# A hybrid trunk layer on one core: later turns of gated tiles, and queries and chain outputs turned by DMA

## The chip, the core and the metric

The kernel runs on one core of a Trainium2 chip. The metric is the device time of one execution in microseconds (us); for the kernel before it is the median of three runs. The profile comes from one more execution, taken by the hardware profiler. Engines are named as in the profile: PE (TensorE, matrix products and transposes), DVE (VectorE), ACT (ScalarE), POOL (GpSimd) and SP (SyncE, which here only issues loads).

## The reference, cut to what matters

The layer takes x (256 x 2048, float32) through three sub-layers, each with an RMS norm before and after it: a SwiGLU half-step, a mixer of two gated linear attentions, a second SwiGLU half-step.

```python
def swiglu(x, w_gate, w_up, w_down):              # w_gate, w_up: 2048 x 5504
    return (jax.nn.silu(x @ w_gate) * (x @ w_up)) @ w_down

proj = u @ w_in
(g_q, g_k, g_v, g_out, g_code, h_q, h_f, h_i, h_out, z_gla, z_hgrn) = jnp.split(proj, offsets, axis=-1)
...
o_gla = merge_heads(rms_norm(o_gla, gla_norm)) * jax.nn.silu(g_out)       # 4 heads, dk 128, dv 256
...
o_hgrn = merge_heads(rms_norm(o_hgrn, hgrn_norm)) * jax.nn.silu(h_out)    # 8 heads, dk 128, dv 128
merged = (jax.nn.sigmoid(z_gla + b[0]) * (o_gla @ w_branch_gla)
          + jax.nn.sigmoid(z_hgrn + b[1]) * (o_hgrn @ w_branch_hgrn))
return merged @ w_out
```

Both attentions are causal recurrences with a decay for each key channel: S_t = diag(a_t) S_{t-1} + k_t v_t^T, o_t = S_t^T q_t.

## The kernel before, in words

**Tiles.** The 256 rows are two row tiles t = 0, 1 of 128 partitions; columns go in blocks of CB = 512. A product needs its left operand transposed, with the contracted dimension on the partitions, so whatever is a left operand later has to be turned (128x128 transposes, four for a 128x512 tile). Every float32 operand is split in a high part (`hi`, rounded, by ACT) and the rest (`lo`, by DVE; `split_into`, line 152), and a product is three matmuls on PE (`mm3`, line 157, lines 159 to 161). Weights come as chunks of 128x1024 elements: `raw` loaded by SP (line 135), `whi` by ACT (line 153), `wlo` by DVE (line 155), in a ring of five buffers. Some pairs of chunks are multiplied by a scheme of seven products (`seven`, line 263), which saves PE work and costs DVE sums.

**Two ways to turn a tile.** By PE: `transpose4` (line 397) writes four transposes (line 399) to a PSUM tile, from which ACT copies or splits. By DMA: `turn` (line 406) has ACT part the two 16-bit halves of each float32 into `halves` (line 410) and issue a transposing DMA from ACT's own queue (line 414); `joined` (line 417, instruction at 419) has ACT put the halves together again. Before the change DMA turns the gated tiles of both SwiGLU stages (`finish`, line 719) and the merged tiles of the mixer (`merge`, line 1262); PE turns all else, the queries (`transposed`, line 847) and the attentions' outputs (line 1006) among them.

**The order of the work.** The code is one long list of products, with small steps between them. `Side` (line 43) keeps two lists of generators. After a chunk of products the code calls `side.pump()`: each generator of the light list makes one step (to its next `yield`), and up to two of the heavy list, which holds the attention chains, make one as well. In a pair block called with `late` the heavy ones step only while the light list is empty; otherwise, with two or more of them, at every second pump. In `gemm_pair` (line 331) heavy steps stop (`side.full`) from the step before the first `seven` to the end of the block. `side.flush()` runs the light list out, `side.until(...)` pumps until something is there. Each engine then works through its own queue in a fixed order.

**The mixer** (line 800). One block for the GLA query, one for the code and the first HGRN query (line 1134), then pair blocks: GLA key and value, value and gate, gate and HGRN forget, HGRN value and gate of group 0, query and forget of group 1, value and gate of group 1. Six attention chains (`attention`, line 891) run beside them: GLA for t = 0, 1 (two output blocks each), HGRN group 0 and group 1 for t = 0, 1 (one each). A chain waits for its operands, goes through seven levels, for t = 0 turns its key (`ke`), then for each output block makes the products, the state, the norm and the gated output `on` (line 1001); two steps later PE turns `on` and it is split into `oT` (lines 1012, 1013). Then come the gate blocks and branches: `done("g")` (line 1247) pumps until the GLA outputs are there, gate block, two GLA branch blocks, `done("h")` (line 1253, group 0 alone), three gate blocks with two GLA branch blocks in between, then all chains are run out (line 1278). Four HGRN branch blocks (line 1280) each spawn `merge` for both row tiles: a product and a sum on DVE (lines 1264, 1265), four pumps, the turn, a load of a tile kept in DRAM (`h<-away`, line 1269, also from ACT's queue), four pumps, `joined`, one pump, the split. The output projection (`out_proj`, line 552, PSUM tiles `acc`) reads the result.

**The SwiGLU stages** (`ffn`, line 693). Eleven column blocks of gate and up products; for each, `finish` makes the gated tile, and one step later turns it, six steps later joins it in `hT`. The down projection (`down_proj`, line 605) reads `hT` as its left operand in 43 chunks for each half of the columns; after the second chunk it runs the light list out (line 662).

## Time and profile before

| | us |
|---|---|
| median of 3 runs | 2063.67 (2061.78 to 2066.02) |
| the profiled execution | 2067.03 |
| its span, first to last instruction | 2065.2 |

A line of the profile's groups or waits names an engine, a line of the kernel, the operation and the tiles (out<-in, with buffer numbers left out). Busy time is the time in which an engine carries out instructions; "idle before" is how long it stood still just ahead of them, and the arrow names what it waited for. `ACTq` and `SPq` are the queues of ACT and SP issuing a DMA; such issues are not counted as busy. Matmuls overlap on PE, so the distance between their starts, not the duration of one, is what PE pays.

### The profile page before, as it was taken

The numbers are of one execution on the slowest core, as the hardware profiler recorded it, in microseconds if no ns is written. First come the engines' busy times: TensorE is split into PE (matmuls) and PEld (weight loads), VectorE is DVE, ScalarE is ACT, GpSimd is POOL, SyncE is SP. The second block draws the span as 40 slices with busy tenths as digits, with TensorE's granted clock in tenths as the row PEclk, the third lists the DMA queues.
The fourth block names the chain that finished last, engine by engine and source line by source line (L and its number), as shares of the span: only waits on it lengthen the run. The fifth ranks groups of instructions, "written<-read, shape, count | busy, mean of one in ns | idle before, by whom it ended". The sixth has DMA issues, their size and how long they took to land. (4 is left out here: it accounts for less than half of the span.)

```text
span 2065.2 us, 28965 instructions
## 1 busy us (share of the span) xinstructions
PE 2046.2 (99%) x10299; PEld 1697.1 (82%) x10299; DVE 1864.5 (90%) x2195; ACT 1324.6 (64%) x1734; POOL 41.0 (2%) x87
## 2 busy tenths in 40 slices
PE   9999999999999999999999999999999999999998
PEld 8888888888888888878888887788888888888886
DVE  7999999998999889989999895578999999999897
ACT  7666666666666576576655556566666666766663
POOL 1000000000000100000000000010000000000000
PEclk9999999999999999999999999999999999999999
DMA  8777677677767566565665668956767767776664
GB/s 258 217 208 244 191 221 219 209 225 210 232 187 235 155 199 220 155 191 175 184 197 186 191 219 197 255 160 195 235 193 215 220 213 228 222 234 199 208 195 145
DMA packets 255129, 425.60 MB, mean 206 GB/s; under 512 B 71988, under 2 KB 80375, under 8 KB 254984
## 3 DMA queue, kind: packets, MB, share of 16 engines
q1 hardware_dynamic: 195472, 401.80, 61.8%
q10 hardware_dynamic: 59512, 21.94, 5.8%
q8 instruction: 81, 1.33, 0.3%
q14 instruction: 64, 0.52, 0.1%
HBM read 406.11 MB, written 4.19 MB: 199 GB/s over the span
## 5 line engine op out<-in xcount | busy, mean ns | idle before, releaser
L155 DVE TENSOR_TENSOR wlo<-raw,whi 128x1024 fp32r<-128x1024 f32 (+3 forms) x494 | 578.3, 1186 | 76.0 <-ACT whi L153 72.3
L153 ACT ACTIVATE whi<-raw 128x1024 fp32r<-128x1024 f32 (+3 forms) x494 | 499.3, 1025 | 193.3 <-PE c L160 59.0
L159 PE MATMUL c<-whi,xhi 128*128 128x512 f32 (+1 forms) x1270 | 494.8, 390 | 0.7 <-ACT whi L153 0.7
L161 PE MATMUL c<-wlo,xhi 128*128 128x512 f32 (+1 forms) x1270 | 491.5, 387 | 0.0
L160 PE MATMUL c<-whi,xlo 128*128 128x512 f32 (+1 forms) x1270 | 491.3, 387 | 0.0
L245 DVE TENSOR_TENSOR wlo<-raw,whi 128x1024 fp32r<-128x1024 f32 x256 | 304.0, 1219 | 36.0 <-ACT whi L284 22.8
L159 PEld LDWEIGHTS c<-whi,xhi 128*128 128x128 f32 x1270 | 238.4, 188 | 48.3 <-ACT whi L153 1.0
L161 PEld LDWEIGHTS c<-wlo,xhi 128*128 128x128 f32 x1270 | 238.4, 188 | 47.7 <-DVE wlo L245 0.2
L160 PEld LDWEIGHTS c<-whi,xlo 128*128 128x128 f32 x1270 | 238.5, 188 | 46.2
L284 ACT ACTIVATE whi<-raw 128x1024 fp32r<-128x1024 f32 x128 | 135.2, 1056 | 219.2 <-DVE raw L245 115.0
L245 DVE TENSOR_TENSOR wsuml<-wsum,wsumh 128x1536 fp32r<-128x1536 f32 x128 | 224.3, 1753 | 7.6 <-ACT wsumh L286 7.6
L161 PE MATMUL c<-wlo,hkhi 128*128 128x512 f32 x542 | 211.0, 389 | 0.0
L159 PE MATMUL c<-whi,hkhi 128*128 128x512 f32 x542 | 211.0, 389 | 0.0
L160 PE MATMUL c<-whi,hklo 128*128 128x512 f32 x542 | 210.9, 389 | 0.0
L282 ACT ACTIVATE wsumh<-wsum 128x1024 fp32r<-128x1024 f32 x128 | 134.6, 1052 | 84.2 <-DVE wsum L245 60.2
L280 ACT ACTIVATE whi<-raw 128x1024 fp32r<-128x1024 f32 x128 | 134.6, 1051 | 60.0 <-PE c L160 43.4
L245 DVE TENSOR_TENSOR wsum<-raw,raw 128x1024 f32<-128x1024 f32 x128 | 156.3, 1221 | 12.0 <-DMA raw<-in_ffn_w_down_dram 9.6
L161 PEld LDWEIGHTS c<-wlo,hkhi 128*128 128x128 f32 x542 | 101.7, 188 | 21.6 <-DVE wlo L245 0.3
L160 PEld LDWEIGHTS c<-whi,hklo 128*128 128x128 f32 x542 | 101.7, 188 | 21.0
L159 PEld LDWEIGHTS c<-whi,hkhi 128*128 128x128 f32 x542 | 101.7, 188 | 21.0
L245 DVE TENSOR_TENSOR c<-c,psum 128x512 f32<-128x512 f32 x135 | 87.4, 694 | 6.7 <-PE c L161 6.5
L245 DVE TENSOR_TENSOR wsum<-raw 128x512 f32<-128x512 f32 x128 | 88.4, 691 | 3.5
(326 smaller groups left out, 3192.2 us busy)
## 6 DMA issues: line engine op xcount, KB each, us to landing
raw<-in_ffn_w_down_dram SPq DMA_DIRECT2D x120, 512.0 KB, 4.8
raw<-in_w_in_dram SPq DMA_DIRECT2D x104, 512.0 KB, 4.5
raw<-in_ffn_w_gate_dram SPq DMA_DIRECT2D x90, 512.0 KB, 4.6
raw<-in_ffn_w_up_dram SPq DMA_DIRECT2D x90, 512.0 KB, 4.5
raw<-in_ffn_w_gate_dram SPq DMA_DIRECT2D x140, 256.0 KB, 3.9
raw<-in_ffn_w_up_dram SPq DMA_DIRECT2D x140, 256.0 KB, 3.7
raw<-in_w_in_dram SPq DMA_DIRECT2D x128, 256.0 KB, 3.6
raw<-in_ffn_w_down_dram SPq DMA_DIRECT2D x104, 256.0 KB, 4.0
```

The lines of the kernel that those rows point to most:

```text
L153: last[0] = nc.scalar.activation(hi, src, AF.Copy)
L155: nc.vector.tensor_tensor(lo, src, hi.bitcast(F32), op=ALU.subtract)
L159: nc.tensor.matmul(ps, lhsT=xhi, rhs=whi, start=start, stop=False)
L160: nc.tensor.matmul(ps, lhsT=xlo, rhs=whi, start=False, stop=False)
L161: nc.tensor.matmul(ps, lhsT=xhi, rhs=wlo, start=False, stop=stop)
L245: return nc.vector.tensor_tensor(o, x, y, op=op)
L280: nc.scalar.activation(ahi, ra, AF.Copy)
L282: nc.scalar.activation(hi[:, 0:2, :], wsum[:, 0:2, :], AF.Copy)
L284: nc.scalar.activation(bhi, rb, AF.Copy)
```

## The change

- `turn` is parted in `halved` (the 16-bit halves, on ACT or DVE) and `turn` (the DMA alone); `joined` can run on either engine as well.
- `finish`: the turn begins one step later for t = 0 and three for t = 1, and `joined` comes eight steps after the turn, not six.
- `down_proj`: no flush after the second chunk of the first half; a pump after each chunk instead, and a flush at the half's end.
- `turned_into`: a query tile is turned by DMA, 2 + 2t steps after it is spawned, and joined six steps after that. It takes the place of `transposed` for the GLA queries and the first HGRN queries.
- `attention`: all outputs but those of HGRN group 1 are turned by DMA one step after `on`, and joined and split four steps later.
- `merge`: both copies run on DVE, `halved` at once; the DMA goes out 3 + 2t steps later, `joined` and the split follow six steps after that.

```diff
-    def turn(src, halves):
+    def move(eng, dst, src):
+        if eng is nc.scalar:
+            nc.scalar.activation(dst, src, AF.Copy)
+        else:
+            eng.tensor_copy(dst, src)
+
+    def halved(src, halves, eng=nc.scalar):
 
         w = src.shape[-1]
         halves = halves.bitcast(U16)[:, :2 * w]
-        nc.scalar.activation(halves.rearrange("p (h f) -> p h f", h=2),
-                             src.bitcast(U16).rearrange("p (f h) -> p h f", h=2), AF.Copy)
+        move(eng, halves.rearrange("p (h f) -> p h f", h=2),
+             src.bitcast(U16).rearrange("p (f h) -> p h f", h=2))
+        return halves
+
+    def turn(halves):
         turned = work.tile([P, 8, P], U16, tag="tmp", name=nm("turned"), bufs=3)
-        turned = turned[:, :2 * w // P, :]
+        turned = turned[:, :halves.shape[-1] // P, :]
         nc.scalar.dma_start_transpose(turned, halves)
         return turned
...
@@ down_proj
-                if not hf and kt == 1:
-                    side.flush()
+                if not hf:
+                    side.pump()
                 kt += 1
             if not hf:
+                side.flush()
...
@@ finish
-                turned = turn(s[:, :w], fwork.tile([P, CB], F32, tag="halves", name=nm("halves")))
-                for _ in range(6):
+                for _ in range(1 + 2 * t):
+                    yield
+                halves = fwork.tile([P, CB], F32, tag="halves", name=nm("halves"))
+                turned = turn(halved(s[:, :w], halves))
+                for _ in range(8):
                     yield
...
@@ mixer
+            def turned_into(dst, src, before):
+
+                for _ in range(before):
+                    yield
+                turned = turn(halved(src, blk("halves")))
+                for _ in range(6):
+                    yield
+                joined(tiles4(dst), turned)
+                mark(dst)
...
-                    side.spawn(transposed(src, dsts[-1]))
+                    side.spawn(turned_into(dsts[-1], src, 2 + 2 * t) if dma else
+                               transposed(src, dsts[-1]))
...
@@ attention
                     yield
-                    yield
-                    tp = ps_tile()
-                    transpose4(tp, on)
+                    if (br, b0) == ("h", 1):
+                        yield
+                        tp = ps_tile()
+                        transpose4(tp, on)
+                    else:
+                        tp = on
+                        turned = turn(halved(on, blk("halves")))
+                        for _ in range(4):
+                            yield
+                        joined(tiles4(on), turned)
...
-            qT = spawn_T(qs, "qT")
+            qT = spawn_T(qs, "qT", True)
...
-            hqT = spawn_T(hqs, "hqT")
+            hqT = spawn_T(hqs, "hqT", True)
...
@@ merge
-                for _ in range(4):
+                halves = halved(s, blk("halves"), nc.vector)
+                for _ in range(3 + 2 * t):
                     yield
-                turned = turn(s, blk("halves"))
+                turned = turn(halves)
                 nc.scalar.dma_start(m, away[t][n])
-                for _ in range(4):
+                for _ in range(6):
                     yield
-                joined(tiles4(s), turned)
-                yield
+                joined(tiles4(s), turned, nc.vector)
```

## The prediction, made before the changed kernel was run

> **What bounds the kernel now.** I read the page first: who is busy, and how much is left.

> ```profile
> span 2065.2 us, 28965 instructions
> ...
> PE 2046.2 (99%) x10299; PEld 1697.1 (82%) x10299; DVE 1864.5 (90%) x2195; ACT 1324.6 (64%) x1734; POOL 41.0 (2%) x87
> ```

> PE stands idle for 2065.2 - 2046.2 = 19.0 us in all, so it is the bound. Time can come from two places alone: instructions taken off PE, and those 19 us. The waits of PE (total, times, longest) and two stretches of the windows view (length, then busy time of PE, PEld, DVE, ACT) say where the idle time is.

> ```profile
> PE acc L159 <- ACT whi L153: 4.4, 2, 2.8
> ...
> PE acc L161 <- DVE wlo L155: 1.1, 2, 0.5
> PE c L159 <- ACT whi L153: 0.7, 1, 0.7
> PE p L161 <- DVE wsuml L245: 0.6, 1, 0.6
> ```

> ```profile
> 700.00:1238.00 538.00, 537.59 (x3542) 444.34 (x3541) 493.96 (x676) 338.93 (x528) 14.43 (x22) 1.00 0.61 190
> 1253.00:1310.00 57.00, 50.83 (x218) 39.97 (x217) 30.54 (x36) 33.58 (x37) 0.00 (x0) 1.00 0.96 199
> ```

> In the mixer's long middle (700 to 1238 us) PE misses 0.4 us of 538. From 1253 to 1310 us, where the hgrn branch's products end, `merge` runs and the output projection begins (tile `acc`), it misses 57.00 - 50.83 = 6.2 us. The timeline of that place shows why ("ACTq" is ACT's queue issuing a DMA):

> ```profile
> 1284.15 3.28 ACTq L414 DMA_TRANSPOSE turned<-halves  x1
> 1287.47 2.01 ACT L153 ACTIVATE whi<-raw 128x1024 fp32r<-128x1024 f32 x2 [3.36 <-issue]
> 1288.58 0.50 PE L159 MATMUL acc<-whi,xhi 128*128 128x512 f32 x1 [2.81 <-ACT whi L153]
> ...
> 1299.15 5.05 ACTq L414 DMA_TRANSPOSE turned<-halves  x1
> ```

> Twice ACT's queue is held by issuing a transpose (3.28 and 5.05 us), the split of the next weight chunk (`whi`) stands behind it, and PE waits for that split. So `merge`'s turns on ACT cost PE time here, and nowhere else does a wait of PE reach 1.5 us.

> **The change, part by part.** *Transposes taken off PE.* The first queries of both attentions are two tiles each, the outputs of the four chains (GLA two blocks for each row tile, HGRN group 0 one) six tiles: 10 tiles of four 128x128 transposes, 40 in all.

> ```profile
> 741.78 1.09 PE L399 MATMUL ps<-ident,hq 128*128 128x128 f32 x8
> 742.62 0.47 PE L159 MATMUL c<-whi,xhi 128*128 128x512 f32 x1
> ```

> The 1.09 us run to the end of the last one; instructions overlap on PE, and what counts is the distance of starts: the next product starts 742.62 - 741.78 = 0.84 us after the first of 8 transposes, 0.105 us for each. 40 x 0.105 = 4.2 us. PE has no slack in this stretch, so this part is worth **-4.2 us**; its bounds are close, since a transpose taken out can neither save more than its turn nor, with 0.4 us idle in 538, hide in a pause.

> [...]

> *What comes instead, on ACT.* A turn is `halves` (L410), the issue (L414), `joined` (L419); the `copy` of the four query tiles out of PSUM (L853) goes.

> ```profile
> L419 ACT ACTIVATE sz<-turned 128x1024 uint16<-128x1024 uint16 x8 | 10.5, 1361 | 2.2 <-DMA turned<-halves 2.1
> L410 ACT ACTIVATE halves<-sz 128x1024 uint16<-128x1024 uint16 x8 | 8.4, 1049 | 5.8 <-DVE wlo L155 2.7 <-DVE sz L1265 1.8 <-DVE xlo L155 1.3
> L853 ACT COPY hqT<-ps 128x512 f32<-128x512 f32 x4 | 2.1, 585 | 0.0
> ```

> ```profile
> L414 ACTq DMA_TRANSPOSE turned<-halves x52: 1242/1288/5047, 45.8 to 1836.3; - x52
> ...
> DMA to landing us min/median/max: 3.1/5.2/9.6
> ```

> 10 x (1.05 + 1.29 + 1.36) - 4 x 0.585 = 34.7 us on ACT, which is busy 339 of 538 us in that stretch: cover enough on average. The outputs of both row tiles turn in one step, so two transposes stand back to back; the second can hold ACT up to 5.05 us. PE feels that only where ACT's splits are less than that ahead. Queued behind it are the splits of the next chunks, and behind those PE. Bounds 0 and one such hold, 5 us; I take **+0.5**, near 0, because PE waits for such a split ("PE c L159 <- ACT whi") once in the run, 0.7 us. The new tiles (`halves` from the same pool of 33) may wait for a free one; no row shows such a wait, 0.

> *merge.* Its `halves` and `joined` go from ACT to DVE, 8 each, and the two row tiles' turns are set two steps apart instead of together. ACT in the 57 us: 33.6 busy, and its queue issues 8 transposes, two of them at 3.28 and 5.05 and six at no less than the row's least, 1.24: 15.8 us or more. That is 49 of 57 before the 8 issues of `h<-away`: ACT is nearly full, and in the wrong moments. The move takes 8 x 1.05 + 6 x 1.36 = 16.6 off it (two `joined` lie later), the spacing up to 8.3 - 2 x 1.24 = 5.9. ACT then needs 27 to 33 of the 51 us that PE needs. DVE gets 14 copies of 1024 16-bit elements that the trace doesn't show; nearest rows in the same stretch:

> ```profile
> L155 DVE TENSOR_TENSOR wlo<-raw,whi 128x1024 fp32r<-128x1024 f32 x16 | 19.1, 1221 | 21.6 <-ACT whi L153 21.6
> L1265 DVE TENSOR_TENSOR sz<-h,sz 128x512 f32<-128x512 f32 x8 | 5.3, 685 | 0.0
> ```

> At 1.22 us (same count of elements) that is 17.1, DVE 47.6 of 51; at 0.69 it is 9.6, DVE 40 of 51. I take 1.22, the row with the same elements. DVE then is nearly full, so I leave 1.7 of the 6.2 us standing: **-4.5 us**, bounds 0 (the wait moves to DVE) and -6.2.

> [...]

> *Later turns of the gated tiles (both SwiGLU stages).* `halves` comes one or three steps later, `joined` two more; the flush after the second chunk of the down projection becomes a step per chunk and a flush at the half's end. This ends ACT's waits for landing:

> ```profile
> ACT hT L419 <- DMA turned<-halves: 14.3, 13, 3.9
> ```

> Of PE's waits only the rows of 0.7 and 0.6 us could lie in these stages, so the 14.3 are idle time of an engine with slack: **0** (bound -1.3). The last tile is read from chunk 36 on, its turn needs 12 steps: cover holds; without it PE would wait for one landing, 5.2 us.

> *Order: the chains fall behind.* This is the hidden cost. An output needed 2 steps after `on`, now it needs 5 (one, the turn, four more). A pair block called with `late` leaves the chains five steps: `full` is set from entry 5 of its 13 on. Counting by the code: before, GLA's two outputs used steps 2 and 4 of the block HQ+HF and group 0 began in step 5. Now the first takes all five, the second the steps of the next block and two empty turns of `done("g")`; group 0 begins a block later, so its output is not even turned when `done("h")` comes (10 turns with no product between them), and group 1's last level, `ke`, products and output all stand behind the last gate block, where before only the output's transposes stood. What this costs depends on whether a queue follows the code's order. It doesn't strictly:

> ```profile
> 1202.28 0.39 PE L976 MATMUL ps<-hv,sc 128*128 128x128 f32 x2
> 1202.42 0.48 PE L159 MATMUL c<-whi,xhi 128*128 128x512 f32 x1
> ...
> 1203.44 0.39 PE L160 MATMUL c<-whi,xlo 128*128 128x512 f32 x1
> 1203.66 0.38 PE L979 MATMUL ps<-state,hqT 128*128 128x128 f32 x2
> ```

> L976 and L979 follow each other in the code; products of the gate block were put between them while L979's state was copied. At `done("h")`, then, the next block's splits and products can stand ahead of the turned tiles. For the tail I use group 0's chain:

> ```profile
> 1023.61 0.60 PE L399 MATMUL ps<-ident,hkT 128*128 128x128 f32 x4
> ...
> 1027.60 1.05 PE L976 MATMUL ps<-h,sc 128*128 128x128 f32 x8
> 1028.49 1.06 PE L986 MATMUL ps<-h,ke 128*128 128x128 f32 x8
> ```

> ```profile
> 1034.79 1.12 DVE L1001 SCALAR_TENSOR_TENSOR on<-ps,r,h 128x128 f32<-128x128 f32 x4
> ```

> From `ke` to the last `on` 1035.9 - 1023.6 = 12.3 us, of which some 2.7 are the block's own step between (12 products at 0.23); with the last level before and the output's transposes after it some 12.5 us. PE's own work in it: 32 products at 0.11 (8 from 1027.60 to 1028.49) and 12 transposes, 4.8 us. Cover: the first half of each of the four hgrn branch blocks reads group 0 alone, 24 products at 0.22 us (1203.44 to 1203.66) = 5.3 us in each. Bounds 0 (two blocks' halves cover it) and 12.5 - 4.8 = 7.7 (none); I take **+1.0**, near 0, because the rows just above show products slid under such a chain.

> **Sum.** -4.2 + 0.5 - 4.5 + 0 + 1.0 = **-7.2 us**. The profiled execution took 2067.03 us (span 2065.2 and 1.8 around it) and would take 2059.8; the median of the three runs, 2063.67, lies 3.4 below it, so I forecast 2063.67 - 7.2 = **2056.5 us**.

> **The rivals.** *The code's order holds at done("h")* (slower). ACT's splits for the third gate block stand behind group 0's turned outputs, and that block has no chunk prepared (`ready` is empty). Then PE idles from group 0's products to the first split: 1035.9 - 1027.6 = 8.3 us less 3.5 of PE's own products, two `halves` 2.1, two issues 2.6, landing 5.2, two `joined` 2.7, split 1.05: 18.4 us, so 2063.67 - 7.2 + 18.4 = 2074.9. It decides once fewer splits are ahead of the outputs in ACT's queue than the chain has steps of 2.7 us. For it: ten empty turns. Against it: the interleaving above, and ACT's slack in the same place:

> ```profile
> 1076.00:1086.00 10.00, 10.00 (x161) 7.90 (x161) 9.43 (x21) 5.30 (x6) 0.53 (x1) 1.00 0.82 264
> 1086.00:1096.00 10.00, 10.00 (x131) 8.10 (x120) 10.00 (x21) 2.66 (x3) 0.00 (x0) 1.00 0.58 163
> ```

> ACT is busy 8 of 20 us, and the new work is about 11. [...] Chance 0.15, partly hidden cases (above 2068) included.

> *Given back* (no change). The transposes' 4.2 us come, but `merge` only trades ACT for DVE (its 6.2 us stay) and the tail costs 3 instead of 1.0: 2063.67 - 4.2 + 0.5 + 3 = 2063.0. For it: DVE at 47.6 of 51. Chance 0.20.

> *The forecast*: with all 6.2 us of `merge` gone and nothing lost, 2063.67 - 10.4 = 2053.3; with 3 of them gone and 3 lost in the tail, 2063.67 - 4.2 + 0.5 - 3 + 3 = 2060.0. Chance 0.65. That the change leaves PE's work as it is can't be: the 40 transposes stand in the code of before and not after.

> **How the numbers follow.** Repeated runs spread by 0.2%, about what can be told from no change; 0.2% is 4.1 us. The forecast's cases are nearly all beyond it: faster 0.65; the second rival is within it: 0.20; the first slower: 0.15. The runs of before lie up to 2.4 us from their median; with that on either side the range goes from 2053.3 - 2.3 = 2051 to 2066, above the second rival's 2063.0, and leaves the first out.

> **What would show it.** Right: L399 loses 40 transposes; the waits "acc <- whi" shrink from 4.4 to about 1; no issue of L414 near `merge` above 3 us; PE's idle total near 15. Wrong: a PE wait of many us near 1085 (`done("h")`), or a new one near 1240 to 1255 for `oT` or `state`; DVE copies in `merge` over 1.3 us with "acc <- wlo" waits; PE waits in the SwiGLU stages, where I expect none.

## The result and the profile after

| | before | after |
|---|---|---|
| median, four runs each, taken together | 2063.85 us | 2076.95 us |
| ratio, 95% interval | | 1.0066 [1.0054, 1.0078] |
| the profiled execution | 2067.03 us | 2076.57 us |
| its span | 2065.2 us | 2074.6 us |

The ratio is that of a kernel's times to the times of the kernel before in the same session; in the sessions of the experiments below the median of before is 2062.9 to 2063.9 us. The changed kernel is slower, by 13.1 us in the medians. The two profiled executions differ by less, 9.5 us, because that of before lies 3 us above its median. First the page of after, against the page shown of before:

```profile
span 2074.6 us, 28922 instructions
...
PE 2050.1 (99%) x10259; PEld 1698.2 (82%) x10259; DVE 1879.9 (91%) x2211; ACT 1329.0 (64%) x1734; POOL 39.4 (2%) x87
```

The 40 transposes are gone (10259 instructions, not 10299), and yet PE is busy for 3.9 us longer and idle for 24.5 us, 5.5 more. The waits of PE (total, times, longest) give new names to the idle time:

```profile
PE ps L399 <- DVE hkT L959: 2.7, 1, 2.7
...
PE mm L161 <- DVE wlo L155: 2.0, 1, 2.0
PE ps L399 <- DVE on L1025: 1.9, 2, 1.0
...
PE acc L159 <- DVE sz L1295: 1.2, 1, 1.2
```

The old row "acc <- ACT whi" is gone, as forecast. Three waits for pieces of the attention chains have come. Where they lie, the windows of after show (length, then busy time of PE, PEld, DVE, ACT, POOL; the first number without a count is PE's granted clock, as a share of full speed):

```profile
700.00:1238.00 538.00, 533.10 (x3457) 435.68 (x3456) 491.06 (x665) 354.29 (x524) 10.46 (x18) 1.00 0.64 195
1238.00:1256.00 18.00, 12.98 (x71) 10.87 (x69) 8.46 (x18) 8.72 (x28) 2.41 (x4) 0.81 0.19 59
1253.00:1310.00 57.00, 55.17 (x232) 44.83 (x231) 41.49 (x53) 21.37 (x24) 0.00 (x0) 0.96 0.77 197
```

and the second of these stretches before the change:

```profile
1238.00:1256.00 18.00, 18.00 (x85) 14.98 (x84) 15.32 (x19) 10.49 (x14) 0.00 (x0) 1.00 0.61 191
```

From 700 to 1238 us PE now misses 4.9 us where it missed 0.4; the largest piece is the 2.0 us for `wlo`, at 1057 us. From 1238 to 1256 us PE now stands idle for 5.0 of 18 us, and it runs at a mean clock of 0.81. This is the end of the last chain. PE's timeline of after there (start, duration, instruction, and in brackets the idle time before it with its releaser):

```profile
1237.56 1.15 PE L950 MATMUL ps<-hqT,hkT 128*64 128x64 f32 x16
1241.39 1.12 PE L399 MATMUL ps<-ident,hkT 128*128 128x128 f32 x4 [2.68 <-DVE hkT L959]
1242.30 1.91 PE L1000 MATMUL ps<-hv,sc 128*128 128x128 f32 x8
...
1248.71 1.10 PE L399 MATMUL ps<-ident,on 128*128 128x128 f32 x4 [0.98 <-DVE on L1025]
1250.71 0.33 PE L399 MATMUL ps<-ident,on 128*128 128x128 f32 x1 [0.91 <-DVE on L1025]
1250.80 0.48 PE L159 MATMUL mm<-whi,oT 128*128 128x512 f32 x1
```

The last level (L950), the end of `kT` (L399 on `hkT`), the products and the two outputs follow one another with nothing between them, and the hgrn branch's first product starts at 1250.80, behind all of them but the last three transposes. The first and longest wait is DVE's: the scaling of `hkT` stands in its queue behind four products of the gates, as DVE's timeline of after shows.

```profile
1238.28 2.72 DVE L1064 SCALAR_TENSOR_TENSOR sz<-c,r,sz 128x512 f32<-128x512 f32 x4
1240.91 0.42 DVE L959 TENSOR_TENSOR hkT<-hkT,tot 128x256 f32<-128x256 f32 x1
```

Product by product (the same index of L159, L160 and L161 in both traces) after is 2.69 us ahead of before at 1207 us and 11.78 behind at 1256 us: the tail costs 14.5 us. Of these, 5.0 are idle time and about 3.4 the clock (two stretches of 3.413 us at half speed, told below); the other 6.1, by subtraction, are work of the chain that before had already done. Behind it 4.1 come back up to the end of `merge`, and 2.4 are lost again near 1445 us, in the second SwiGLU, where PE waits 1.6 us for `wsuml`; e1 and e7 below, with the same code in that place, have no such wait above 0.7 us, so the cause of this piece is open.

### The profile page after: what moved, and what is told of

It reads as the page before. It is cut to its first block, busy times and chain, and to the rows that moved or that the text cites. A ratio compares the mean times of both kernels' runs of the same rounds, so it can differ in the third digit from the quotient of the medians.

```text
span 2074.6 us, 28922 instructions
## 1 busy us (share of the span) xinstructions
PE 2050.1 (99%) x10259; PEld 1698.2 (82%) x10259; DVE 1879.9 (91%) x2211; ACT 1329.0 (64%) x1734; POOL 39.4 (2%) x87
## 5 line engine op out<-in xcount | busy, mean ns | idle before, releaser
L153 ACT ACTIVATE whi<-raw 128x1024 fp32r<-128x1024 f32 (+3 forms) x494 | 498.8, 1025 | 216.3 <-PE c L160 88.8
L155 DVE TENSOR_TENSOR wlo<-raw,whi 128x1024 fp32r<-128x1024 f32 (+3 forms) x494 | 578.9, 1187 | 49.2 <-ACT whi L153 46.5
L159 PE MATMUL c<-whi,xhi 128*128 128x512 f32 (+1 forms) x1270 | 494.3, 389 | 0.6 <-ACT whi L284 0.6
L161 PE MATMUL c<-wlo,xhi 128*128 128x512 f32 (+1 forms) x1270 | 491.1, 387 | 0.5 <-DVE wlo L155 0.3
L160 PE MATMUL c<-whi,xlo 128*128 128x512 f32 (+1 forms) x1270 | 491.3, 387 | 0.0
L245 DVE TENSOR_TENSOR wlo<-raw,whi 128x1024 fp32r<-128x1024 f32 x256 | 304.9, 1220 | 27.6 <-ACT whi L280 14.6
L161 PEld LDWEIGHTS c<-wlo,xhi 128*128 128x128 f32 x1270 | 238.4, 188 | 49.3 <-DVE wlo L245 1.4
L159 PEld LDWEIGHTS c<-whi,xhi 128*128 128x128 f32 x1270 | 238.4, 188 | 48.9 <-ACT whi L284 1.0
L160 PEld LDWEIGHTS c<-whi,xlo 128*128 128x128 f32 x1270 | 238.5, 188 | 46.4
L245 DVE TENSOR_TENSOR wsuml<-wsum,wsumh 128x1536 fp32r<-128x1536 f32 x128 | 224.4, 1753 | 5.3 <-ACT wsumh L286 5.3
L159 PE MATMUL c<-whi,hkhi 128*128 128x512 f32 x542 | 210.9, 389 | 0.0
L161 PE MATMUL c<-wlo,hkhi 128*128 128x512 f32 x542 | 210.8, 389 | 0.0
L160 PE MATMUL c<-whi,hklo 128*128 128x512 f32 x542 | 210.8, 389 | 0.0
L245 DVE TENSOR_TENSOR wsum<-raw,raw 128x1024 f32<-128x1024 f32 x128 | 156.3, 1221 | 17.3 <-DMA raw<-in_ffn_w_down_dram 11.6
L161 PEld LDWEIGHTS c<-wlo,hkhi 128*128 128x128 f32 x542 | 101.8, 188 | 21.2
L160 PEld LDWEIGHTS c<-whi,hklo 128*128 128x128 f32 x542 | 101.7, 188 | 21.1
L159 PEld LDWEIGHTS c<-whi,hkhi 128*128 128x128 f32 x542 | 101.7, 188 | 21.0
L245 DVE TENSOR_TENSOR c<-c,psum 128x512 f32<-128x512 f32 x135 | 89.4, 695 | 8.5 <-PE c L161 8.0
L245 DVE TENSOR_TENSOR wsum<-raw 128x512 f32<-128x512 f32 x128 | 88.5, 691 | 3.7
```

Source lines behind the costliest of these rows:

```text
L153: last[0] = nc.scalar.activation(hi, src, AF.Copy)
L155: nc.vector.tensor_tensor(lo, src, hi.bitcast(F32), op=ALU.subtract)
L159: nc.tensor.matmul(ps, lhsT=xhi, rhs=whi, start=start, stop=False)
L160: nc.tensor.matmul(ps, lhsT=xlo, rhs=whi, start=False, stop=False)
L161: nc.tensor.matmul(ps, lhsT=xhi, rhs=wlo, start=False, stop=stop)
L245: return nc.vector.tensor_tensor(o, x, y, op=op)
```

## The experiments

**Is it the order or the DMA?** The theory: the outputs' five steps make the last chain late (order). The rival: the transposing DMAs, their landing and their copies on ACT cost the time themselves. The first pair does the outputs the old way in the changed kernel, and the new way alone in the kernel before.

```diff
 # e1: after, outputs back on PE
-                    if (br, b0) == ("h", 1):
-                        yield
-                        tp = ps_tile()
-                        transpose4(tp, on)
-                    else:
-                        tp = on
...
+                    yield
+                    tp = ps_tile()
+                    transpose4(tp, on)
```

> The changed kernel, but all attention outputs turned by PE again, two steps after `on`; queries, merge and gated tiles as changed. Theory A (order: the five steps of an output push the chains back, and PE stands idle and at half clock where their end has nothing beside it): the tail at 1238 to 1256 us and the wait at 1057 us go, the 24 transposes of the outputs come back (2.5 us): 2063.85 - 1.7 (queries) - 4 (merge), some 2057 to 2061. Theory B (the DMA way itself costs, through ACT's queue and the copies, wherever it stands): four of the ten tiles still go that way, 2063.85 + 0.4 x 13 = about 2069. Theory C (merge's copies on DVE cost): nothing of the loss goes, 2075 or more.

> The kernel before with one part of the change alone: the outputs of four of the six chains turned by DMA in five steps. A: the tail and the wait at 1057 us as in the changed kernel, less 2.5 us of transposes: 2063.85 + 13 - 2.5, about 2074, and half-clock windows near 1060 and 1240 us. B: six of ten tiles, 2063.85 + 0.6 x 13 = 2072, spread over the mixer without half-clock windows. C: no loss, about 2061.

Measured: e1 2061.12 us against 2063.83, ratio 0.9987 [0.9978, 0.9997]; e2 (the block that e1 takes out, put into before) 2077.89, ratio 1.0066 [1.0051, 1.0081]. The whole loss comes with the outputs, and the other three parts together gain a little. e2 has the same three waits (2.7, 2.0 and 1.9 us) and the same jump in the tail (14.4 us); its time is some 4 us above what theory A gave. This still leaves order and DMA together, so the next kernel has the five steps without any DMA.

```diff
 # e9: before
-                    yield
-                    yield
+                    for _ in range(2 if (br, b0) == ("h", 1) else 5):
+                        yield
                     tp = ps_tile()
                     transpose4(tp, on)
```

> The kernel before, and its outputs still go through PE, but those of the four chains wait five steps of their chain (not two) after the gated output before they are transposed, as many as the changed kernel's outputs take; no DMA, no copy, nothing else is changed. If the order alone makes the loss (the chains of the last block get their steps too late and end behind the last gate product): slower than before by 8 to 14 us (2072 to 2078), a jump of 10 us or more between 1237 and 1256, and the same three waits of PE there (for DVE's hkT, state, on). If the DMA, its landing or the copies on ACT make it: within 2 us of before.

Measured: 2074.47 us, ratio 1.0051 [1.0038, 1.0064]: 10.6 us slower, with the work of before and nothing but three more steps of waiting. PE's timeline of e9 at `done("h")` (first two rows) and in the tail:

```profile
1085.95 1.02 PE L399 MATMUL ps<-ident,on 128*128 128x128 f32 x4 [1.18 <-DVE on L1001]
1088.03 0.33 PE L399 MATMUL ps<-ident,on 128*128 128x128 f32 x1 [1.06 <-DVE on L1001]
...
1242.74 0.66 PE L399 MATMUL ps<-ident,hkT 128*128 128x128 f32 x4 [2.69 <-DVE hkT L935]
...
1250.29 1.11 PE L399 MATMUL ps<-ident,on 128*128 128x128 f32 x4 [0.99 <-DVE on L1001]
1252.30 0.33 PE L399 MATMUL ps<-ident,on 128*128 128x128 f32 x1 [0.90 <-DVE on L1001]
```

In the tail the waits are those of after to within 0.01 us. The order is shown to be the cause of most of the loss, 10.6 of 13.1 us, though not in the same places throughout: from 1010 to 1110 and from 1235 to 1310 us, where after's four stretches of half clock lie, e9 has one (at 1243.3), waits 0.6 us at 1057 us and not 2.0, and waits 2.7 us at `done("h")` (the two rows above and 0.45 for `state`), where after does not wait. The other side of the same test keeps the DMA and takes the steps away, in two ways: with `joined` one step after the turn (e3), and with the output as a small generator of its own in the light queue, while its chain goes on after one step (e10).

```diff
 # e3: after
-                        for _ in range(4):
-                            yield
+                        yield
                         joined(tiles4(on), turned)
 # e10: after
+                def turned_out(on, t, b):
+                    yield
+                    turned = turn(halved(on, blk("halves")))
+                    for _ in range(5):
+                        yield
+                    joined(tiles4(on), turned)
+                    scaled_out(on, t, b)
...
+                        side.light.append(turned_out(on, t, b))
+                        yield
```

> The changed kernel, but `joined` stands one step after the output's turn instead of four, so that an output takes two steps, as many as by PE before; the same instructions, only the order differs. A: the chains keep their old places, the tail and the wait at 1057 us go, the transposes stay off PE: 2063.85 - 4.2 - 4 + 0 to 2, so 2056 to 2060. B and C: as the changed kernel, 2075 to 2078.

> The changed kernel, but an output that is turned by DMA goes on as a small piece of its own, which steps at every pump (halves copied and turned one pump later, joined and scaled five pumps after that), while its chain goes on to the next output after one step. If the chains' steps are the loss: the tail's jump of 14.5 us goes, no wait of over 1.5 us for hkT or on there, and the time is 2057 to 2063. If the landing waits in the queues of ACT and DVE make it, as the 6 us that the kernel with two steps kept over the one with PE's outputs may say: 2065 to 2072.

Measured: e3 2067.14, ratio 1.0012 [1.0001, 1.0022]; e10 2063.63, ratio 1.0004 [0.9994, 1.0014]. In both the tail is full again, as this window of e10 shows:

```profile
1236.00:1256.00 20.00, 20.00 (x94) 16.61 (x94) 18.04 (x23) 10.54 (x13) 0.00 (x0) 1.00 0.61 188
```

e10 ends 0.6 us above the first range of its expectation. e3 missed its own by some 7 us. One reason stands in its timeline (three engines): with `joined` so close behind the turn, a late landing holds ACT, DVE behind it, and then PE.

```profile
940.38 1.36 ACT L408 ACTIVATE on<-turned 128x1024 uint16<-128x1024 uint16 x1 [2.39 <-DMA turned<-halves]
...
942.13 0.89 DVE L1043 SCALAR_TENSOR_TENSOR oT<-on,ncol,oT 128x256 fp32r<-128x256 f32 x2 [2.63 <-ACT oT L1042]
...
947.87 0.50 PE L161 MATMUL p<-wlo,xhi 128*128 128x512 f32 x1 [2.54 <-DVE wlo L245]
```

ACT stands still for the landing, DVE for ACT's `oT`, and the weights' low part that PE needs is queued behind both. This costs PE 2.5 us. In `merge` e3 also has a mean clock of 0.94 from 1262 to 1322 us, where e1 has 1.00; by an estimate from this (0.06 of 60 us) it costs up to 3.6 us, and the rest of what e3 missed is not accounted for.

So of the 15.8 us between e1 and after, 13.3 come back in e10, with every DMA kept. The last 2.5 go with the DMA way itself, although e10 has 2.5 us of transposes less on PE than e1; e10's profile has a wait of 1.7 us for `wlo` near 1057 us and half-clock stretches at 1060.5 and 1313.1 (its mean clock over the span is 0.997, e1's 0.999), but which of its pieces brings them was not taken apart.

**How much of it is PE's clock?** PE's products start every 0.23 us, but behind the pause at 1057 us, for instance, they start every 0.43 (after's timeline):

```profile
1059.95 0.76 PE L161 MATMUL mm<-wlo,oT 128*128 128x512 f32 x1 [1.99 <-DVE wlo L155]
1060.51 0.63 PE L159 MATMUL mm<-whi,oT 128*128 128x512 f32 x1
1060.94 0.63 PE L160 MATMUL mm<-whi,oT 128*128 128x512 f32 x1
```

Four stretches of 3.413 us at a granted clock of 0.5 lie in after, from 1060.0, 1240.9, 1251.2 and 1305.8 on, and in the profile of before none between 4.2 and 2059 us. In the first of them PE is busy throughout and has 8 products, where at 0.23 us each there would be 15. By an estimate from the granted 0.5 such a stretch costs half its length, 1.7 us, where PE is busy throughout; the four together cost up to 6.8. e5 fills the pauses of the tail with products that nobody reads; the kernel then has 4.3 us more to do on PE.

```diff
 # e5: after
+            def fill(n):
+                ps, hi = ps_tile(), oT["h", 0, 0][0]
+                for _ in range(n):
+                    nc.tensor.matmul(ps, lhsT=hi[:, 0, :], rhs=hi.rearrange("p k c -> p (k c)"),
+                                     start=True, stop=True)
...
+                    if (br, b0) == ("h", 1):
+                        fill(11)
...
+                        fill(4)
```

> The changed kernel with 19 products added in the tail that nobody reads: 11 behind group 1's last level, where PE stands idle 2.7 us, 4 ahead of each of its two output turns. They add 4.3 us of PE work and no wait. If the half clock after these pauses is a cost of its own (two stretches of 3.41 us at 0.5, 1.7 us each), the stretches near 1241 and 1251 us go and the time is 2076.95 - 3.4 = 2073.5, although PE has more to do. If the pauses alone cost, the time is 2077 or, where a filler is late, up to 2079.

Measured: 2070.8 us, ratio 1.0038 [1.0024, 1.0052]. That is 6.2 us less than after in the medians, and 5.2 less if each is taken against before in its own session (7.9 and 13.1 us slower). The tail of e5:

```profile
1236.00:1256.00 20.00, 19.05 (x114) 15.56 (x115) 11.22 (x21) 10.77 (x29) 2.41 (x4) 1.00 0.23 71
```

No half clock is left there, and the jump of the tail is 11.5 us. The fillers stand in time that was idle (5.0 us of it have become 0.95), so they cost next to nothing, and they give back the two stretches, up to 3.4 us. Over the whole span e5's mean clock is 0.997, after's 0.996. In this tail, with its pauses filled, the clock is up (1.00 in the window above, where after has 0.83); the rest of the gain is not accounted for.

**Why did `merge` not gain its 4.5 us?** The theory: DVE now waits in its own queue for the landing, ahead of the weights' low parts. Four kernels: the merge part alone (e4), with `joined` back on ACT (e6), with `joined` twelve pumps behind the turn (e11), and the gated tiles alone, which leave `merge` as it was (e7).

```diff
 # e4: before, with merge as in after; e6: e4 and
-                joined(tiles4(s), turned, nc.vector)
+                joined(tiles4(s), turned)
 # e11: e4 and
-                for _ in range(6):
+                for _ in range(12):
                     yield
                 joined(tiles4(s), turned, nc.vector)
```

> The kernel before with merge's part of the change alone (both copies on DVE, the turns of the two row tiles two steps apart). A: the waits of PE at 1276 to 1306 us shrink from 6.2 us to about 2: 2059 to 2061. C: 2066 or more. B: as A.

> The kernel before with merge's part of the change, but `joined` left on ACT; only `halves` moves to DVE, and the turns are spaced as in the change. In the run of merge's part alone DVE stood at `joined` until the turn landed, and the splits `wlo` of the output projection behind it. If that is what ate merge's gain, the waits 'acc <- DVE wlo' (5.4 us there) fall under 2 us and the time is 2064.7 - 4 = about 2060. If DVE's load or the spacing is the cause, it stays at 2064 to 2066.

> The kernel before with the later turns of the gated tiles and the pumps of the down projection alone. PE hardly waits in the SwiGLU stages, so 2063.8, less or more 1.5 us. In the changed kernel 2.4 us were lost near 1445 us, in the second SwiGLU's second pair: if the later turns cause that, 2065 to 2066.

> The kernel before with the merge part alone, and the joining twelve pumps after the turn instead of six. If DVE's wait for the landing, which stood in its queue ahead of the weights' low parts, gave the merge part's gain away: no DVE sz wait for turned left (17.5 us in six pieces with six pumps), PE's wait for DVE's wlo in the merge zone under 2 us (5.4), and 2059 to 2062. If the wait moves on to another row once more, as it did with the joining on ACT: 2063 to 2066, and that row is named by the trace (the first products of the out projection, which need the last blocks joined, are the nearest one).

Measured: e4 2064.67 us, ratio 1.0006 [0.9997, 1.0016]; e6 2065.46, 1.0016 [1.0007, 1.0025], both above what the theory gave; e11 0.9991 [0.9982, 1.0000], e7 0.9991 [0.9982, 1.0000]. The waits from 1235 to 1330 us, first of e4, then of e6, e11 and e7:

```profile
DVE sz L410 <- DMA turned<-halves: 17.5, 6, 4.4
...
PE acc L161 <- DVE wlo L155: 5.4, 3, 2.2
```

```profile
ACT sz L408 <- DMA turned<-halves: 9.8, 4, 3.9
...
PE acc L159 <- DVE sz L1273: 5.6, 1, 5.6
```

```profile
PE acc L161 <- DVE wlo L155: 4.2, 2, 2.6
...
DVE sz L410 <- DMA turned<-halves: 15.5, 4, 5.2
```

```profile
PE acc L161 <- DVE wlo L155: 1.1, 2, 0.5
...
PE acc L159 <- ACT whi L153: 0.4, 2, 0.2
```

With each edit the landing is waited for on the engine that has the copy, and PE waits behind it; in e6 by way of DVE, whose own wait for a split of ACT lasts up to 6.2 us there. Twelve pumps leave DVE 15.5 of its 17.5 us of waiting, so the distance in pumps is not what decides, and e11's expectation fell; its gain of 1.3 us is at the edge of what can be told. e7's rows are the answer: there `merge` is the old one, and its stall in this execution is 1.5 us, not 5.5. From 1270 to 1325 us PE waits 6.0 us in before and 3.8, 2.8, 2.7 and 1.5 in e2, e9, e8 and e7, all with the old `merge`; in after, e1, e3, e4, e5 and e10, with the changed one, it waits 1.7 to 5.7. The stall that the move was to end was large in the one profiled execution that I had read, and these executions do not tell the two apart. e7 also has no wait near 1445 us, so the later turns do not by themselves cause the loss of after there. What sets the landing in this place stays open.

**The queries.** e8 has the queries' DMA alone, as in the diff above.

> The kernel before with the first queries of both attentions turned by DMA alone: 16 transposes off PE, -1.7 us. In all runs with this part, 1.9 us are lost again near 755 us; if that wait belongs to it, 2063.8, no change; if not, 2062.1.

Measured: 2063.74, ratio 1.0002 [0.9993, 1.0011]. The 16 transposes come off PE, and the offset to before, product by product, then falls back by 1.9 us near 755 us, where ACT's queue has an issue, `joined` and four splits close together and PE waits twice for `wlo`: nothing is gained.

**The best of the parts.** The two parts that did not lose by themselves, gated tiles (e7) and the later `merge` (e11), in the kernel before:

> The kernel before with the two parts that did not lose by themselves: the later turns of the gated tiles (0.9991 alone) and the merge on DVE joined twelve pumps after the turn (0.9991 alone); outputs and queries as before. If the two gains are real and add: 0.998, some 2060, under both kernels. If each of the two is the spread between runs: 0.9995 to 1.0005. Either way no half clock between 1010 and 1260, since the order of the chains is that of the kernel before.

Measured: 2061.14 us against 2063.11, ratio 0.9989 [0.9980, 0.9998]; e1, at 0.9987 [0.9978, 0.9997], says the same. e12 lies between its two expectations, and its mean clock over the span is 0.999, as in before's profile (after's 0.996). Each is faster than the kernel before by 2.0 to 2.7 us, which is less than the 0.2% that the prediction called the least one can tell, though the intervals leave 1 out.

## Why the prediction was wrong

I forecast 2056.5 us with a range of 2051 to 2066, and faster at 0.65; it is 2076.95 and slower. Forecast and result lie 20.3 us apart (-7.2 and +13.1). By the runs of single parts the order makes 9.6 of them, `merge` 5.3, and the transposes, which left PE and gave nothing, 4.2; these come from separate runs and need not add up.

- **The step that failed is "Order: the chains fall behind".** I saw the right mechanism (five steps for two, group 1's chain behind the last gate block) and gave it +1.0 us out of bounds of 0 and 7.7. e9 measures it alone: +10.6. I took the low end because rows at 1202 to 1203 us show products slid between L976 and L979, and reckoned with the hgrn branch's first halves, 5.3 us each, as cover. In the trace of after no such product starts before 1250.80: the code runs all chains out (line 1278 of the kernel before) ahead of the first product of that branch (line 1280). The rows that I relied on show products of a block that was already under way; the branch's products come only after the last step of the chains. With no cover my own upper bound, 7.7, was the value to take, and it would have made the sum about 0 (-0.5). Not all of e9's 10.6 us lie in the tail: 2.7 are waits at `done("h")`.
- **The bound itself was too low, since PE's clock was not in the sum.** The 5.0 us of idle time in the tail lie within my bounds. The 3.4 of half clock that follow them, and 1.7 each at 1060 and 1306, are in no term. In before's profile every clock entry that I quoted reads 1.00, so no row of it showed a price. In after pauses of 2.0 and 2.7 us went with a stretch of half clock, and so did two of 1.0 and 0.9 us close together.
- **A second place was missed.** At 1057 us PE waits for `wlo`, 2.0 us and the clock's 1.7. DVE's timeline of after shows what stands ahead of that `wlo`:

```profile
1055.70 2.73 DVE L1064 SCALAR_TENSOR_TENSOR h<-c,r,h 128x512 f32<-128x512 f32 x4
1058.34 0.42 DVE L225 TENSOR_TENSOR sums<-xhi,xlo 128x256 f32<-128x256 f32 x1
1058.67 1.23 DVE L155 TENSOR_TENSOR wlo<-raw,whi 128x1024 fp32r<-128x1024 f32 x1
```

  They are four products of the gates, as in the tail. With the order alone the wait is 0.6 us (e9), with the DMA and without the late chains 1.7 (e10), so it goes with the DMA way more than with the order; which piece of it does this is open. I had looked for a wait at `done("h")`. There, my slower rival's place, nothing happened in after, as its windows show:

```profile
1076.00:1086.00 10.00, 10.00 (x64) 8.57 (x63) 9.19 (x11) 6.77 (x15) 0.00 (x0) 1.00 0.86 266
1086.00:1096.00 10.00, 10.00 (x51) 8.45 (x50) 6.96 (x14) 5.53 (x16) 2.52 (x4) 1.00 0.65 185
```

  PE is busy without a gap; only e9, with the outputs on PE, waits here (2.7 us). The rival's 2074.9 us is near the result, but by another way, 150 us later in the kernel; its chance of 0.15 was the only one for a loss.
- **Transposes, -4.2.** They did leave PE (10259 instructions). The queries' 1.7 us of them are given back (e8, ratio 1.0002), and the outputs' 2.5 twice over: e10, which has them off PE without the order's price, is 2.5 us slower than e1, which has them on PE. It is not the price of a transpose that decided: e9 loses 10.6 us without any DMA, by the steps.
- **`merge`, -4.5.** Measured alone, +0.8 us within its interval (e4). The 6.2 us came from one execution that took 3.4 us more than its median, which I noted, but charged to nothing. The size of a copy on DVE was wrong as well, in the other direction (groups of after):

```profile
L410 DVE COPY halves<-sz x8: 677/688/692, 1265.7 to 1307.7; 128x1024 uint16<-128x1024 uint16 x8
L410 DVE COPY sz<-turned x8: 747/757/764, 1271.3 to 1317.1; 128x1024 uint16<-128x1024 uint16 x8
```

  They take 0.69 and 0.76 us, not the 1.22 that I took. That they are shorter did not help, because DVE's time went into waiting for the landing, 17.5 us in e4, which was no term either.
- **Gated tiles, 0**: right within what can be told (e7, 0.9991 [0.9982, 1.0000]). That they end ACT's waits for landing was wrong: 14.8 us in after against 14.3.
- **ACT, +0.5**: no wait of PE for a split on ACT above 0.6 us is left in after; the term was small and stayed so.

## What to carry to other kernels

Where chains of small steps share pumps with the main stream, an operation that needs more steps can be paid at the end of the last chain, however cheap it is (here three more steps cost 10.6 us): count the steps up to the point where the main stream has nothing left to emit, and take that tail as uncovered unless the products that should cover it are emitted before it ends. Let such an operation go on by itself while its chain goes on (e10 against after: 13.3 us). And take a stall's size from more than one execution before it becomes a term of a sum.

## What the runs showed of the chip that was not expected

```profile
1237.50:1240.90 3.40, 1.21 (x17) 1.01 (x16) 3.40 (x6) 3.34 (x6) 0.00 (x0) 1.00 0.50 162
1240.90:1244.30 3.40, 2.91 (x14) 2.92 (x15) 1.90 (x4) 1.32 (x3) 0.00 (x0) 0.50 0.10 7
...
1247.80:1251.20 3.40, 1.59 (x8) 1.02 (x8) 2.02 (x8) 1.79 (x9) 1.67 (x3) 0.99 0.00 0
1251.20:1254.60 3.40, 3.40 (x11) 2.65 (x10) 1.64 (x3) 0.69 (x1) 0.00 (x0) 0.50 0.00 0
```

In e10 a piece with 1.68 of 3.40 us of work is followed by half clock, in e4 one with 1.70 is not (first e10, then e4):

```profile
1057.10:1060.50 3.40, 1.68 (x69) 1.16 (x68) 3.40 (x7) 2.97 (x5) 0.00 (x0) 1.00 0.01 2
1060.50:1063.90 3.40, 3.40 (x10) 2.63 (x9) 3.40 (x10) 0.20 (x1) 0.00 (x0) 0.51 0.46 154
```

```profile
1285.60:1289.00 3.40, 1.70 (x8) 1.10 (x7) 3.40 (x5) 0.74 (x1) 0.00 (x0) 1.00 0.93 211
1289.00:1292.40 3.40, 3.40 (x16) 2.81 (x16) 1.24 (x2) 1.69 (x2) 0.00 (x0) 1.00 1.05 206
```

The pieces ahead of after's four stretches have 1.83 to 2.22 us of idle time, and no other piece of after between 10 and 2040 us has more than 1.27; in before, cut along the grid of its own half clock at 2059.06 us, one piece has 1.87 (at 1284), and no half clock follows it. So a pause of 2 us costs 2 us here, or by an estimate with the 1.7 us of a stretch about 3.7 if half clock follows it. In e3, e4 and e6 the mean clock from 1262 to 1322 us is 0.94, in after, with one stretch there, 0.97, so the half clock took about twice as long in them; why it did is open. Where the grid lies differs from run to run (e9's stretch at 1243.3 us is 53.7 steps behind after's at 1060.0), and so may the price of the same pause; that the spread of repeated runs comes from this was not tried.
